# A hybrid encoder layer: the long convolution's decay window is read from a table in DRAM instead of being made on ScalarE

## The chip, the cores and the metric

The kernel runs on one core of one Trainium2 chip. The metric is the device time in microseconds of one execution. Of the kernel before, three executions took 3947.34, 3951.09 and 3955.97 us; the median is 3951.09 us.

The engines are named as the profile names them: PE is the matrix engine, with its weight loads shown apart as PEld; DVE is VectorE, ACT is ScalarE, POOL is GpSimd, and SP is the engine that issues most of the DMA transfers. Rows with the engine SPq or ACTq are DMA issues on those queues.

## The reference, cut to what matters

The layer projects 2048 tokens of 1024 channels, runs two token mixers side by side, a Hyena long convolution and an RWKV-7 scan, merges them with gates, normalises, and ends with a SwiGLU feed-forward part and a second normalisation. The change touches the Hyena filters alone:

```
t = jnp.linspace(0.0, 1.0, L)[:, None]
...                                   # a small sine network gives h: (L, 64)
h = (h @ fw4).reshape(L, HY_ORDER, 2, HY_WIDTH)
deltas = jnp.abs(jnp.linspace(HY_MIN_DECAY, HY_MAX_DECAY, HY_WIDTH))
window = jnp.exp(-t * deltas[None, :])
return h * window[:, None, None, :]
```

There are 2 orders, 2 directions and 512 channels. `window` depends on the position and the channel alone: on no input. `long_conv` convolves a signal of length 2048 with a forward and a backward filter by way of an FFT of length 4096, and adds `d_skip * z`, which the kernel folds into position 0 of the filter.

## The kernel before, in words

The program has these stages in order of time: the input projection with the preparation of the scan (to about 640 us), the scan in 64 chunk steps with the gate columns of the projection woven in (to about 1600 us), the long convolutions (to about 2110 us), the merge of the branches, and the feed-forward part (from about 2490 us). Dense products are made of three matmuls on split operands.

**The convolutions.** 512 channels make 4 blocks of 128, and each is convolved twice (order 0 and 1): eight products, in the order of the list `PRODUCTS`. For a product the filter's spectrum is made first, in eight chunks of four (128 x 128) pieces, by the generator `filters()`. For chunk q of a product:

- PE multiplies the sine network's output with the product's last weight matrix: tile `pg`, four matmuls of 128 x 128 (L1240; each is two passes, so a chunk shows as x8). In chunk 0 a row for the skip term is added (L1242).
- DVE multiplies `pg` with the window chunk, in place (L1244). This runs at raised priority.
- PE makes the first half of the Fourier transform of the result: tile `pf` (L1226, x8).
- ACT copies `pf` to SBUF (L1228) and stores it to the DRAM array `Hd` with a DMA on its own queue (L1229).

Each `yield` of the generator is a piece: "window product" and "transform of the chunk before" alternate, so that the transform of chunk q-1 follows the window product of chunk q. `upto(n)` runs the generator on. The window chunk itself is made on ACT by four exponentials of a row of deltas, each with its own scale column (L1214), one chunk ahead, in one of three buffers of 128 x 512 (ring places 8, 9 and 10).

**Who runs filters().** The first product's eight chunks, and two of the second, are made while the last steps of the scan run (steps 62 and 63) and just behind them; I call the stretch from 1540 to 1616 us the ramp. In it SP also loads the tables of the convolution (`open()` and `taken(k)`: `H3b`, the network's output, and `Fc`, the Fourier table, in four parts of 512 KB each, one part for two chunks), ACT and DVE run the scan's last normalisations (`normed`: squares L867, a root L868, a scaling L872) and the short convolutions (L1183, L1184, L1189). PE then turns the first signal (tile `ph` L1285) and transforms it (`pfz` L1294).

From 1616 us on, product k runs beside the filters of product k+1. A product has eight slots; in slot q PE makes `pz` from the signal's transform and `pz` from the next filter's (both L1309), DVE multiplies the first with the filter's spectrum (`H`, L1339) and with its swapped form (`Hs`, L1340), and PE adds up (`pq`, L1348 and L1349). `H` is a copy on ACT (L1325), and `Hs` is made from it by four small DMAs of 64 KB on SP (L1329, shown as `rg<-rg`). The filters' pieces (called F in `beside`) are put into slots 0, 1, 4, 5, 6 and 7. In slots 3 and 6 SP also reads half of the next product's spectrum back from DRAM (`Vf<-Hd`, L1319, four DMAs of 256 KB). The last filter piece is at about 2020 us.

**What sets the order.** In the scan the order of PE's instructions is written out by hand and the other engines are ordered by a scheduler; in the convolutions PE, ACT, DVE and SP all run in the order in which the code is written. Every DMA of SP and ACT signals one of eight semaphores in turn (named DMAHW0 to DMAHW7 in the program), and each DMA's issue waits until the DMA that last used its semaphore, eight places earlier in the two queues together, has landed.

Of the kernel before, what the change touches and what calls it, by code (L numbers as in the profile page):

```python
# [9 lines left out]
F32 = mybir.dt.float32  # L10
F32R = mybir.dt.float32r
AF = mybir.ActivationFunctionType
# [4 lines left out]
P = 128  # L17
# [5 lines left out]
HT = 4  # L23
# [16 lines left out]
PRODUCTS = [(c + k, o) for c in (0, 2) for o in range(2) for k in range(2)]  # L40
# [59 lines left out]
def shape_consts():  # L100
    f = np.float32
    F, G, M = fft_consts()
    Fz = np.concatenate([F[:64, 0::2], F[:64, 1::2]], 0)
    out = {"c_F": F, "c_Fz": Fz, "c_G": G, "c_M": M, "c_ident": np.eye(128)}
    p = np.arange(128)
    ind8 = np.zeros((128, HP, 8))
    for hp in range(HP):
        ind8[p, hp, hp * 2 + p // 64] = 1
    out["c_ind8"] = ind8
    out["c_ind8T"] = ind8.transpose(2, 1, 0)  # L110
    out["c_bones"] = (p[:, None] // 64 == p[None, :] // 64)
    sm = np.ones((128, 512))
    sm[:, ::CH] = 0
    out["c_smask"] = sm
    i = np.arange(64)
    row, col = i[:, None], i[None, :]

    mb = [row < col, row < col]
    mk = [row < col, row > 63 - col]
    rb = [row <= col, 63 - row >= col]  # L120
    rk = [row <= col, row >= col]
    even = lambda b, k: np.stack([np.concatenate([k[d], b[d]], 0) for d in range(2)], 1)
    odd = lambda b, k: np.stack([np.concatenate([b[d], k[d]], 0) for d in range(2)], 1)
    out["c_maskA"] = np.stack([even(mb, mk), odd(mb, mk)], 1)
    out["c_maskR"] = np.stack([even(rb, rk), odd(rb, rk)], 1)
    t = np.linspace(0.0, 1.0, L, dtype=f)
    w = (f(2.0 * math.pi) * np.arange(L, dtype=f) / f(L)).astype(f)
    fr = np.linspace(1e-4, 15, 16, dtype=f)
    ang = (w[:, None] * fr[None, :]).astype(f)
    feats = np.concatenate([t[:, None], np.cos(ang), -np.sin(ang)], -1).astype(f)  # L130
    n1, n2 = np.arange(64), np.arange(32)
    fwd = (32 * n1[None, :] + n2[:, None])
    bwd = 2048 - 32 * n1[None, :] - n2[:, None]
    bwd[0, 0] = 0
    out["c_feats"] = np.concatenate([feats[fwd.reshape(-1)].T, feats[bwd.reshape(-1)].T], 0)
    out["c_tcol"] = -np.concatenate([t[fwd].T, t[bwd].T], 0)
    mn, mx = math.log(1e-2) / 1.5, math.log(1e-2) / 0.3
    dl = np.abs(np.linspace(mn, mx, 512, dtype=f))
    out["c_delta"] = np.tile(dl[None], (128, 1))
    e0 = np.zeros((1, 128))  # L140
    e0[0, 0] = 1
    out["c_e0"] = e0
    return {k: np.ascontiguousarray(v, dtype=f) for k, v in out.items()}


# [1 line left out]
def lay_out(a):  # L147
# [36 lines left out]
    }  # L184
    o = {k: np.ascontiguousarray(v) for k, v in o.items()}
    o.update(shape_consts())
    return o

class Layer:
# [428 lines left out]


    def ring(self, k):
        return self.cm.tile([P, 512], F32, name="rg", tag=f"rg{k % 14}")

    def chain(self):
        tc, nc, i = self.tc, self.nc, self.i
# [2 lines left out]
        with tc.tile_pool(name="ch", bufs=1, reuse_waits="tile") as s, tc.tile_pool(name="chp", bufs=1, space=PSUM, reuse_waits="tile") as ps:  # L629
# [348 lines left out]
            def until(gen, n):  # L978
                for _ in range(n):
                    yield next(gen)  # L980
# [122 lines left out]
    def open(self):  # L1103
        nc, i = self.nc, self.i
        self.H3 = self.xp1.tile([P, 32, P], F32, name="H3b", tag="xh", bufs=1)
        self.Fc = self.xp1.tile([P, 32, P], F32, name="Fc", tag="xl", bufs=1)
        cu = self.wp.tile([P, 1026], F32, name="cu0", tag="wraw", bufs=2)
        self.Mc = self.wp.tile(self.i["c_M"].shape, F32, name="Mc", tag="wraw", bufs=2)
        self.Fz = [self.wp.tile([P, 8, P], F32, name="Fz", tag="wh", bufs=2) for k in range(2)]
        self.Gc = [self.wp.tile([P, 16, 64], F32, name="Gc", tag="wl", bufs=2) for k in range(2)]  # L1110
        self.turns = dict(w=0, A=0, B=0, H=0, Hs=0)
        self.smalls, self.pieces = {}, 0
        self.spots = [cu[:, 514:1026], self.ring(11)]
        self.tcol = self.load(self.fp, "c_tcol")
        self.e0 = self.load(self.fp, "c_e0")
        cw = self.load(self.fp, "conv")
        self.cw, self.cb = cw[:, :, 0:3], cw[:, :, 3]
        self.small(*PRODUCTS[0])
        self.taken(0)
        self.cus = [cu, self.wp.tile([P, 528], F32, name="cu1", tag="ex")[:, 0:514]]  # L1120
        self.conv, self.convs = self.shorts(), {}
        self.z0 = self.short(0)
        for k in range(2):
            nc.sync.dma_start(self.Fz[k], i["c_Fz"][:, 8 * k:8 * k + 8])
        nc.sync.dma_start(self.Mc, i["c_M"])
        for k in range(2):
            nc.sync.dma_start(self.Gc[k], i["c_G"][:, 16 * k:16 * k + 16])
# [5 lines left out]


    def next(self, name):
        first, n = dict(w=(8, 3), A=(12, 2), B=(0, 2), H=(2, 3), Hs=(5, 3))[name]
        k = self.turns[name]
        self.turns[name] = k + 1
        return self.ring(first + k % n).rearrange("p (a b) -> p a b", b=P)

    def small(self, c, o):
        nc, i = self.nc, self.i
        cs = slice(P * c, P * c + P)
        new = lambda n, sh: self.fp.tile(sh, F32, name=n, tag=n, bufs=2)
        fw4, delta, skip = new("fw4", [P, P]), new("delta", [P, P]), new("skip", [1, P])
        for d in range(2):
            nc.sync.dma_start(fw4[64 * d:64 * d + 64], i["fw4"][:, o, d, cs])
        nc.sync.dma_start(delta, i["c_delta"][:, cs])
        nc.sync.dma_start(skip, i["skip"][:, o, cs])
        self.smalls[c, o] = fw4, delta, skip  # L1150

# [52 lines left out]
    def filters(self):  # L1206
        nc = self.nc
        mm = nc.tensor.matmul
        ahead = None

        def window(delta, q):
            w = self.next("w")
            for j in range(4):
                nc.scalar.activation(w[:, j], delta, AF.Exp, scale=self.tcol[:, 4 * q + j:4 * q + j + 1])  # L1214
            return w

        for i, (c, o) in enumerate(PRODUCTS):
            fw4, delta, skip = self.smalls.pop((c, o))
            if i + 1 < 2 * HT:
                self.small(*PRODUCTS[i + 1])  # L1220

            def spec(q, g):
                ps, tag, bufs = self.fps
                p = ps.tile([P, 4, P], F32, name="pf", tag=tag, bufs=bufs)
                for j in range(4):
                    mm(p[:, j], self.Fc[:, 4 * q + j], g[:, j], start=True, stop=True)  # L1226
                u = self.spots[q % 2].rearrange("p (a b) -> p a b", b=P)
                nc.scalar.copy(u, p)  # L1228
                nc.scalar.dma_start(self.Hd[i, 4 * q:4 * q + 4].rearrange("n p c -> p n c"), u)  # L1229

            last = None
            for q in range(8):
                if ahead is None:
                    ahead = window(delta, q)
                g, ahead = ahead, None
                ps, tag, bufs = self.fps
                p = ps.tile([P, 4, P], F32, name="pg", tag=tag, bufs=bufs)
                for j in range(4):
                    n = 4 * q + j
                    mm(p[:, j], self.H3[:, n], fw4, start=True, stop=n != 0)  # L1240
                    if n == 0:
                        mm(p[:, j], self.e0[0:1], skip[0:1], start=False, stop=True)  # L1242
                with self.tc.high_priority(offset=2 * FIRST):
                    nc.vector.tensor_tensor(out=g, in0=p, in1=g, op=ALU.mult)  # L1244
                if q < 7:
                    ahead = window(delta, q + 1)
                elif i + 1 < 2 * HT:
                    ahead = window(self.smalls[PRODUCTS[i + 1]][1], 0)
                yield
                if q > 0:  # L1250
                    spec(q - 1, last)
                    yield
                last = g
            spec(7, last)
            yield
# [621 lines left out]
```

## Time and profile before

| what | value |
|---|---|
| median of three executions | 3951.09 us |
| the profiled execution, its own time | 3947.99 us |
| its span, first to last instruction | 3946.2 us |
| PE busy, DVE busy, ACT busy | 3801.3 us, 2346.6 us, 1456.8 us |
| exponentials of the window, L1214 | 256 instructions, 82.9 us on ACT |
| window products, L1244 | 64 instructions on DVE, 43.0 us |
| swapping DMAs, L1329 | 256 of 64 KB |
| HBM read, written | 369.52 MB, 144.70 MB |

The profile is of one execution, 3.1 us shorter than the median. A row of stages gives, for each engine, how long it was busy in a stretch of time, then the granted clock of PE as a share of full speed, the share of time that the DMA engines were busy, and the bytes moved in GB/s. A row of waits gives who waited for whom: the time in total, how often, and the longest. A row of the timeline gives start, duration, engine, line, operation and tiles, and in brackets the idle time ahead of it and what ended that.

### The profile page before, as it was taken

What the parts mean: (1) busy time and instruction counts of PE and PEld (TensorE: products, weight loads), DVE (VectorE), ACT (ScalarE), POOL (GpSimd) and SP (SyncE); (2) the same over time, 40 slices, a digit from 0 to 9 for tenths busy, and PEclk for the clock granted to TensorE, in tenths of its full rate; (3) what the DMA queues carried; (4) which work ended last, traced back from release to release, by engine and by line L of the source; (5) the groups of instructions that cost most, each with busy time, mean ns of one, the idle gap of its engine ahead of it and who ended that gap; (6) DMA issues with size and microseconds to landing.
All of it is one profiled execution on the core that took longest, in us unless ns stands there. A gap on an engine that the chain in (4) does not pass through costs nothing.

```text
span 3946.2 us, 64945 instructions
## 1 busy us (share of the span) xinstructions
PE 3801.3 (96%) x26152; PEld 3128.1 (79%) x26152; DVE 2346.6 (59%) x3734; ACT 1456.8 (37%) x2851; POOL 93.1 (2%) x139
## 2 busy tenths in 40 slices
PE   8999999999999998899988999999999999999998
PEld 6766557787777787899887999788888878888887
DVE  5466884666667775577676555544444474444444
ACT  3345663333335566655543333211111151111113
POOL 0000001111010100000000000000000000000000
PEclk9999999999999999899999999999999999999999
DMA  4556878677777777545555443411111142111111
GB/s 140 173 167 172 222 212 247 193 225 206 216 221 223 215 209 216 128 124 141 138 148 180 130 126 110 155 48 49 49 50 51 49 139 69 49 48 48 49 48 43
DMA packets 426420, 535.43 MB, mean 136 GB/s; under 512 B 137268, under 2 KB 305725, under 8 KB 423365
## 3 DMA queue, kind: packets, MB, share of 16 engines
q1 hardware_dynamic: 365703, 459.91, 40.1%
q10 hardware_dynamic: 54528, 54.59, 4.5%
q0 software_dynamic: 5888, 16.78, 1.6%
q8 instruction: 206, 3.38, 0.4%
q14 instruction: 95, 0.78, 0.1%
HBM read 369.52 MB, written 144.70 MB: 130 GB/s over the span
## 4 chain that ended last, share of the span: by engine, by line
PE 51%; DVE 3%; DMA 2%; ACT 1%; issue 1%; SPq 0%; ACTq 0%; DVEq 0%
PE pg L205 4%; PE pg L203 4%; PE pu L203 4%; PE pu L204 4%; PE pg L204 4%; PE pu L205 4%; PE pd L203 4%; PE pd L205 4%; PE pd L204 4%; PE pz L1309 2%; PE pm L203 1%; PE pm L204 1%; PE pm L205 1%; PE po L204 1%; PE po L205 1%; PE po L203 1%
## 5 line engine op out<-in xcount | busy, mean ns | idle before, releaser
L203 PE MATMUL acc<-xh,wh 128*128 128x512 f32 x1376 | 577.3, 420 | 9.4 <-ACT xh L198 8.4
L204 PE MATMUL acc<-xl,wh 128*128 128x512 f32 x1376 | 547.0, 398 | 3.9 <-DVE xl L199 3.8
L205 PE MATMUL acc<-xh,wl 128*128 128x512 f32 x1376 | 547.0, 398 | 0.8 <-DVE wl L199 0.8
L1814 DVE TENSOR_TENSOR acc<-pd,acc 128x1024 f32<-128x1024 f32 x320 | 387.6, 1221 | 69.3 <-PE pd L205 63.6
L198 ACT CAST fwh<-raw 128x1024 fp32r<-128x1024 f32 x132 | 138.6, 1050 | 704.6 <-PE pg L204 487.5
L203 PEld LDWEIGHTS acc<-xh,wh 128*128 128x128 f32 x1376 | 261.6, 190 | 120.4 <-issue 47.9
L1842 DVE TENSOR_TENSOR h<-pu,sg 128x512 f32<-128x512 f32 x88 | 60.9, 692 | 476.6 <-PE pu L205 470.8
L204 PEld LDWEIGHTS acc<-xl,wh 128*128 128x128 f32 x1376 | 262.3, 191 | 63.5 <-DVE xl L199 6.5
L205 PEld LDWEIGHTS acc<-xh,wl 128*128 128x128 f32 x1376 | 261.9, 190 | 62.6 <-DVE wl L199 2.1
L203 PE MATMUL pd<-fwh,hh 128*128 128x512 f32 x704 | 275.6, 391 | 2.8 <-DVE acc L1812 2.4
L205 PE MATMUL pd<-fwh,hl 128*128 128x512 f32 x704 | 274.9, 390 | 0.0
L204 PE MATMUL pd<-fwl,hh 128*128 128x512 f32 x704 | 274.8, 390 | 0.0
L203 PE MATMUL pu<-fxh,fwh 128*128 128x512 f32 x704 | 274.3, 390 | 0.5 <-ACT fxh L1728 0.5
L203 PE MATMUL pg<-fxh,fwh 128*128 128x512 f32 x704 | 274.1, 389 | 0.2 <-DVE fxl L1729 0.2
L205 PE MATMUL pg<-fxh,fwl 128*128 128x512 f32 x704 | 274.2, 389 | 0.0
L205 PE MATMUL pu<-fxh,fwl 128*128 128x512 f32 x704 | 274.1, 389 | 0.0
L204 PE MATMUL pu<-fxl,fwh 128*128 128x512 f32 x704 | 274.0, 389 | 0.0
L204 PE MATMUL pg<-fxl,fwh 128*128 128x512 f32 x704 | 273.9, 389 | 0.0
L199 DVE TENSOR_TENSOR fwl<-raw,fwh 128x1024 fp32r<-128x1024 f32 x132 | 161.1, 1221 | 166.6 <-ACT fwh L198 162.7
L199 DVE TENSOR_TENSOR wl<-wraw,wh 128x512 fp32r<-128x512 f32 (+1 forms) x217 | 169.3, 791 | 138.7 <-ACT wh L198 132.1
L198 ACT CAST wh<-wraw 128x512 fp32r<-128x512 f32 (+1 forms) x217 | 150.2, 704 | 221.2 <-PE acc L204 176.7
L203 PEld LDWEIGHTS pd<-fwh,hh 128*128 128x128 f32 x704 | 132.0, 188 | 41.0 <-DVE acc L1814 12.2
(290 smaller groups left out, 7490.4 us busy)
## 6 DMA issues: line engine op xcount, KB each, us to landing
wraw<-in_w_in SPq DMA_DIRECT2D x130, 512.0 KB
ABp<-ABd SPq DMA_DIRECT2D x64, 512.0 KB
raw<-in_fg SPq DMA_DIRECT2D x44, 512.0 KB
raw<-in_fu SPq DMA_DIRECT2D x44, 512.0 KB
raw<-in_fd SPq DMA_DIRECT2D x44, 512.0 KB
ud<-ev ACTq DMA_DIRECT2D x84, 256.0 KB
ABd<-AB SPq DMA_DIRECT2D x32, 512.0 KB
gated<-ev SPq DMA_DIRECT2D x64, 256.0 KB
```

Of the source, the lines that this page charges most:

```text
L198: nc.scalar.copy(hi, src)
L199: nc.vector.tensor_tensor(out=lo, in0=src, in1=hi.bitcast(F32), op=ALU.subtract)
L203: mm(ps, ah, bh, start=start, stop=False)
L204: mm(ps, ah, bl, start=False, stop=False)
L205: mm(ps, al, bh, start=False, stop=stop)
L1309: mm(p[:, j], Mc[:, 0 if 4 * q + j == 0 else 3], v[:, j], start=True, stop=True)
L1814: tt(out=acc[t], in0=pf, in1=acc[t], op=ALU.add)
L1842: tt(out=h, in0=put, in1=sg, op=ALU.mult)
```

## The change

The window is computed on the host from constants alone and passed as a DRAM array `c_win` of 4 x 128 x 32 x 128 numbers (8.4 MB); `filters()` reads chunk q of channel block c from it with one DMA of 256 KB on SP (128 rows of 2 KB). The first two chunks are asked for at the generator's start, and then the window product of a chunk is followed by the DMA for the chunk two further on; the list `todo` runs over all 64 chunks without a break between products. There are four buffers in place of three: ring place 14, which nothing used before, is the fourth. The window's 256 exponentials, the scale columns (`c_tcol`), the deltas (`c_delta`, one small DMA for each product) and the row `c_e0` with a single 1 go; row 0 of the identity stands in for the last.

```
-    out["c_tcol"] = -np.concatenate([t[fwd].T, t[bwd].T], 0)
+    tcol = -np.concatenate([t[fwd].T, t[bwd].T], 0)
...
-    out["c_delta"] = np.tile(dl[None], (128, 1))
-    e0 = np.zeros((1, 128))
-    e0[0, 0] = 1
-    out["c_e0"] = e0
+    out["c_win"] = np.exp(tcol[None, :, :, None] * dl.reshape(4, 1, 1, 128))
...
     def ring(self, k):
-        return self.cm.tile([P, 512], F32, name="rg", tag=f"rg{k % 14}")
+        return self.spot(k % 14)
+
+    def spot(self, k):
+        return self.cm.tile([P, 512], F32, name="rg", tag=f"rg{k}")
...
-        first, n = dict(w=(8, 3), A=(12, 2), B=(0, 2), H=(2, 3), Hs=(5, 3))[name]
+        spots = dict(w=(8, 9, 10, 14), A=(12, 13), B=(0, 1), H=(2, 3, 4), Hs=(5, 6, 7))[name]
...
-        nc.sync.dma_start(delta, i["c_delta"][:, cs])
...
-        def window(delta, q):
+        def window(c, q):
             w = self.next("w")
-            for j in range(4):
-                nc.scalar.activation(w[:, j], delta, AF.Exp, scale=self.tcol[:, 4 * q + j:4 * q + j + 1])
-            return w
+            nc.sync.dma_start(w, self.i["c_win"][c, :, 4 * q:4 * q + 4])
+            ahead.append(w)
+
+        for _ in range(2):
+            window(*todo.pop(0))
...
             for q in range(8):
-                if ahead is None:
-                    ahead = window(delta, q)
-                g, ahead = ahead, None
+                g = ahead.pop(0)
...
                     if n == 0:
-                        mm(p[:, j], self.e0[0:1], skip[0:1], start=False, stop=True)
+                        mm(p[:, j], self.ident[0:1], skip[0:1], start=False, stop=True)
...
-                if q < 7:
-                    ahead = window(delta, q + 1)
-                elif i + 1 < 2 * HT:
-                    ahead = window(self.smalls[PRODUCTS[i + 1]][1], 0)
+                if todo:
+                    window(*todo.pop(0))
```

PE's instructions stand in the same order in both programs. The two queues that change are ACT and SP.

ACT in the ramp, kernel before: between the third and the fourth copy of a transform (`cu<-pf`, `rg<-pf`, L1228) stand the last step's squares (`sq`), roots (`vr`) and scalings (`y`), the window's exponentials (`rg<-delta`) and the changes of ACT's function table.

```order
L1228 COPY cu_16347<-pf 128x512
L1214 ACT_TABLE_LOAD
L1214 ACTIVATE rg<-delta,k_c_tcol 128x128
L891 ACTIVATE yo<-pgt,k_gn_b,k_gn_w 128x64 x2
L867 ACTIVATE sq,vr<-y,nm 128x64 x4
L1229 DMA Hd<-cu_16347 128x4x128
L868 ACT_TABLE_LOAD
L868 ACTIVATE vr<-vr,eps 128x4
L1214 ACT_TABLE_LOAD
L1214 ACTIVATE rg<-delta,k_c_tcol 128x128
L872 ACTIVATE y<-y,nm,vr 128x64 x4
L1228 COPY rg<-pf 128x512
```

The same two copies in the changed kernel (line numbers shift by a few):

```order
L1228 COPY cu_16347<-pf 128x512
L1229 DMA Hd<-cu_16347 128x4x128
L892 ACTIVATE yo<-pgt,k_gn_b,k_gn_w 128x64 x2
L1228 COPY rg<-pf 128x512
L1229 DMA Hd<-rg 128x4x128
```

All exponentials of the window and, over the whole program, 13 of the 48 table loads of ACT are gone (the seven ahead of L1214 and six of the seven ahead of L868), and one is new ahead of a later activation.

SP in the ramp, kernel before: parts 3 and 4 of `H3b` and `Fc` with the scan's last loads (`A`, `gs`, `bn`, `y`).

```order
L915 DMA yrd<-yo 128x4x128
L1131 DMA H3b<-H3d 128x1024
L1132 DMA Fc<-in_c_F 128x1024
L778 DMA A_4634<-ABd 64x4x64 x2
L898 DMA gs<-gsd 128x128
L900 DMA bn<-bond 128x4x128
L859 DMA y<-Yd 128x256
L1131 DMA H3b<-H3d 128x1024
L1132 DMA Fc<-in_c_F 128x1024
L859 DMA y<-Yd 128x256
```

The same place in the changed kernel:

```order
L916 DMA yrd<-yo 128x4x128
L1211 DMA rg<-in_c_win 128x512
L1130 DMA H3b<-H3d 128x1024
L1131 DMA Fc<-in_c_F 128x1024
L779 DMA A_4634<-ABd 64x4x64 x2
L899 DMA gs<-gsd 128x128
L901 DMA bn<-bond 128x4x128
L860 DMA y<-Yd 128x256
L1211 DMA rg<-in_c_win 128x512 x2
L1130 DMA H3b<-H3d 128x1024
L1211 DMA rg<-in_c_win 128x512
L1131 DMA Fc<-in_c_F 128x1024
```

One window read stands ahead of part 3, two more ahead of part 4 of `H3b`, and a fourth between it and part 4 of `Fc`. The windows of chunks 0 to 3 are read earlier, during the scan, and those of chunks 8 to 11 between these rows and the first `Vf<-Hd`. In the convolutions proper 52 window reads stand between the swaps, each behind the transform (on PE) of the chunk whose buffer it takes.

More of the change, by code (lines that the diff above doesn't have):

```diff
@@ L1113, in open @@
         self.spots = [cu[:, 514:1026], self.ring(11)]
-        self.tcol = self.load(self.fp, "c_tcol")
-        self.e0 = self.load(self.fp, "c_e0")
         cw = self.load(self.fp, "conv")
@@ L1135, in next @@
     def next(self, name):
-        first, n = dict(w=(8, 3), A=(12, 2), B=(0, 2), H=(2, 3), Hs=(5, 3))[name]
+        spots = dict(w=(8, 9, 10, 14), A=(12, 13), B=(0, 1), H=(2, 3, 4), Hs=(5, 6, 7))[name]
         k = self.turns[name]
         self.turns[name] = k + 1
-        return self.ring(first + k % n).rearrange("p (a b) -> p a b", b=P)
+        return self.spot(spots[k % len(spots)]).rearrange("p (a b) -> p a b", b=P)
     def small(self, c, o):
@@ L1144, in small @@
         new = lambda n, sh: self.fp.tile(sh, F32, name=n, tag=n, bufs=2)
-        fw4, delta, skip = new("fw4", [P, P]), new("delta", [P, P]), new("skip", [1, P])
+        fw4, skip = new("fw4", [P, P]), new("skip", [1, P])
         for d in range(2):
             nc.sync.dma_start(fw4[64 * d:64 * d + 64], i["fw4"][:, o, d, cs])
-        nc.sync.dma_start(delta, i["c_delta"][:, cs])
         nc.sync.dma_start(skip, i["skip"][:, o, cs])
-        self.smalls[c, o] = fw4, delta, skip
+        self.smalls[c, o] = fw4, skip
     def shorts(self):
@@ L1208, in filters @@
         mm = nc.tensor.matmul
-        ahead = None
-        def window(delta, q):
+        ahead, todo = [], [(c, q) for c, o in PRODUCTS for q in range(8)]
+        def window(c, q):
             w = self.next("w")
-            for j in range(4):
-                nc.scalar.activation(w[:, j], delta, AF.Exp, scale=self.tcol[:, 4 * q + j:4 * q + j + 1])
-            return w
+            nc.sync.dma_start(w, self.i["c_win"][c, :, 4 * q:4 * q + 4])
+            ahead.append(w)
+        for _ in range(2):
+            window(*todo.pop(0))
         for i, (c, o) in enumerate(PRODUCTS):
-            fw4, delta, skip = self.smalls.pop((c, o))
+            fw4, skip = self.smalls.pop((c, o))
             if i + 1 < 2 * HT:
```

## The prediction

> **What bounds the kernel now.** I read the page's busy shares first, then the stretches of time, then who PE waits for in each, then the chain of waits of the two stretches in which the window is made.
>
> ```profile
> span 3946.2 us, 64945 instructions
> PE 3801.3 (96%) x26152; PEld 3128.1 (79%) x26152; DVE 2346.6 (59%) x3734; ACT 1456.8 (37%) x2851; POOL 93.1 (2%) x139
> ...
> 1400.00:1540.00 140.00, 138.76 (x1746) 113.67 (x1746) 90.85 (x240) 93.36 (x273) 6.88 (x10) 0.99 0.69 187
> 1540.00:1616.00 76.00, 57.68 (x507) 51.12 (x504) 35.20 (x74) 55.14 (x141) 0.00 (x0) 0.77 0.70 200
> 1616.00:2030.00 414.00, 393.46 (x3582) 376.77 (x3583) 291.81 (x329) 234.82 (x504) 0.00 (x0) 0.99 0.52 133
> 2030.00:2112.00 82.00, 66.74 (x584) 62.94 (x583) 60.67 (x65) 26.15 (x43) 0.00 (x0) 0.92 0.45 129
> ```
>
> PE is busy nearly throughout, so work taken off ACT is worth only the PE time that waits for it, or that runs at a low clock because of it. In the scan (first stage) PE idles 1.2 of 140 us. In the ramp it idles 18.3 of 76 us and its clock is 0.77. In the convolutions proper it idles 20.5 of 414 us. The last stage holds no window. So the change can act in the ramp and in the 414 us behind it, and nowhere else; in the scan I put it at nothing.
>
> In the ramp the idle time has a shape:
>
> ```profile
> 1556.49 1.38 PE L1240 MATMUL pg<-fw,H3b 128*128 128x128 f32 x8 [3.68 <-DMA H3b<-H3d]
> ...
> 1580.11 2.08 PE L1240 MATMUL pg<-fw,H3b 128*128 128x128 f32 x8 [3.57 <-ACT rg L1228]
> ...
> 1588.44 2.07 PE L1226 MATMUL pf<-rg,Fc 128*128 128x128 f32 x8 [2.65 <-ACT cu L1228]
> 1591.85 2.05 PE L1226 MATMUL pf<-rg,Fc 128*128 128x128 f32 x8 [1.33 <-DVE rg L1244]
> ```
>
> Up to about 1570 us PE waits for transfers and for the scan's chain; from 1575 on it waits for ACT's copies of the transforms, or for a window product that waits for its exponentials. ACT is full there. The next three rows are of 1570 to 1595 us: all of ACT, then L1214 alone, then the roots' line L868 alone.
>
> ```profile
> 1570.00:1595.00 25.00, 24.05 (x62) 0.72 0.52 157
> 1570.00:1595.00 25.00, 10.19 (x21) 0.72 0.52 157
> 1570.00:1595.00 25.00, 3.16 (x4) 0.72 0.52 157
> ...
> L1214 ACT ACTIVATE rg<-delta,k_c_tcol 128x128 f32<-128x128 f32 x48 | 16.5, 395 | 0.5
> L1214 ACT ACT_TABLE_LOAD x7 | 9.0, 1283 | 0.1
> L868 ACT ACT_TABLE_LOAD x6 | 7.7, 1283 | 0.1
> ```
>
> The last three rows are of 1400 to 1620 us. Exponential and root need different tables, and the two alternate, so each pays a load of 1.28 us.
>
> **The change part by part.** *ACT, ramp.* Of ACT's 24.05 us from 1570 to 1595 go L1214's 10.19 (exponentials and three loads) and the two loads on L868, 2 x 1.28 = 2.57: 12.8 us, half of it. A backlog of that size cannot stay: the copies that PE waited for 3.57 and 2.65 us follow their transforms directly (the rows of the order show it), and the 1.33 us behind a late exponential becomes a wait for a transfer. But something is late next, and it is H3b. SP's issues and PE's product from the third part:
>
> ```profile
> 1549.39 0.43 SPq L1131 DMA_DIRECT2D H3b<-H3d  x1
> ...
> 1560.24 0.50 SPq L1131 DMA_DIRECT2D H3b<-H3d  x1
> ...
> 1567.64 0.45 SPq L1131 DMA_DIRECT2D H3b<-H3d  x1
> ...
> 1567.79 1.06 PE L1240 MATMUL pg<-fw,H3b 128*128 128x128 f32 x8
> ...
> 1560.00:1565.00 5.00, 3.14 (x52) 2.82 (x50) 1.68 (x4) 3.49 (x13) 0.00 (x0) 0.84 0.99 297
> 1570.00:1575.00 5.00, 4.29 (x57) 3.91 (x57) 2.56 (x7) 4.95 (x15) 0.00 (x0) 1.00 0.98 317
> 1575.00:1580.00 5.00, 1.16 (x8) 0.97 (x8) 1.87 (x7) 4.96 (x12) 0.00 (x0) 0.77 0.49 140
> ```
>
> Part 2, issued at 1549.39, released PE at 1556.49: 7.1 us for 512 KB with the DMA engines nearly full, as they are to 1575. Part 4 went out at 1567.64; two window reads now stand ahead of it, at 0.45 us an issue, so say 1568.5, landing 7.1 us later, 1575.6. With the third part's read, three windows of 256 KB are in front of it: 0.75 MB at 317 GB/s is 2.5 us, so 1578. The product of 1580.11 therefore starts 2 us earlier, not 3.57. Behind it the waits of 2.65 and 1.33 us and a small one of 0.4 go: 4.4. Together 6.4 us. Bounds: 2 us, if the reads hold up Fc's fourth part (one more window ahead of it) as well; 8.9 us, all that PE idles from 1575 to 1600, if the transfers overlap better than in sequence. The delay of part 3 by one read, 0 to 3.5 us (half of 7.1), I take as inside the 2.5.
>
> *The clock in the ramp.*
>
> ```profile
> 1575.00:1600.00 25.00, 16.06 (x78) 14.38 (x78) 9.40 (x21) 19.83 (x51) 0.00 (x0) 0.66 0.37 107
> 1600.00:1616.00 16.00, 14.76 (x89) 13.30 (x90) 1.91 (x3) 8.66 (x19) 0.00 (x0) 0.66 0.74 165
> ...
> 1605.00:1610.00 5.00, 5.00 (x25) 4.11 (x25) 0.00 (x0) 2.36 (x5) 0.00 (x0) 0.50 1.09 248
> 1610.00:1615.00 5.00, 5.00 (x31) 5.00 (x31) 0.00 (x0) 1.93 (x4) 0.00 (x0) 0.50 0.87 184
> ```
>
> PE works 30.8 us at a clock of 0.66; at full clock that is 30.8 x 0.66 = 20.3 us. So 0 to 10.5 us can be won where the idle gaps go. The rows argue for less than half: from 1605 to 1615 PE has no gap and still runs at 0.50. I take 4. Ramp: 6.4 + 4 = 10.4 us.
>
> The Trainium skill (TensorE: Matmul & The Clock Gate, Part 1: The HAM clock gate) has it that the matrix engine starts at half clock and gets the full clock after a busy window of about 3.4 us. The two rows just shown are against it for this kind of matmul: ten busy us at 0.50. By the rule, closing the gaps would bring back all of it; that is the first rival below.
>
> *ACT, convolutions proper.* What PE waits for in 1616 to 2030 us:
>
> ```profile
> PE pg L1240 <- ACT cu L1228: 4.1, 6, 0.7
> PE pg L1240 <- DVE rg L1244: 2.9, 3, 1.1
> PE pf L1226 <- DVE rg L1244: 1.5, 1, 1.5
> ...
> PE pg L1240 <- ACT rg L1228: 0.7, 1, 0.7
> ...
> L1214 ACT ACTIVATE rg<-delta,k_c_tcol 128x128 f32<-128x128 f32 x212 | 67.7, 391 | 8.6 <-ACT rg L1228 4.5 <-ACT cu L1228 4.0
> ```
>
> ACT loses 67.7 us of 234.8, a quarter, but it idles 43% here. Only copies that stand directly behind four exponentials (4 x 0.32 = 1.3 us) hold PE: 4.1 + 0.7 = 4.8 us. I take 4. The DVE rows are DVE's own queue (transposes ahead of the window product) and stay.
>
> *SP and the transfers.* Added are 64 reads of 256 KB, 16.8 MB, 52 of them behind 1616 us; gone are eight small loads. By bytes there is room: 133 GB/s moved there, and 13.6 MB over 414 us adds 33. By the queue it is closer:
>
> ```profile
> SPq L1329 <- DMA Hd<-rg: 67.1, 17, 6.1
> ...
> SPq L1329 <- DMA Hd<-cu: 33.2, 14, 4.7
> ...
> DVE rg L1340 <- DMA rg<-rg: 11.0, 9, 2.4
> ...
> PE pz L1309 <- DVE rg L1340: 2.7, 2, 2.4
> ...
> 1666.18 4.11 DMA Hd<-cu
> ...
> 1803.54 1.06 PE L1240 MATMUL pg<-fw,H3b 128*128 128x128 f32 x8
> 1811.62 1.06 PE L1240 MATMUL pg<-fw,H3b 128*128 128x128 f32 x8
> ```
>
> SP's swaps wait 100.3 us, 31 times, for a spectrum store that used their semaphore eight places before: 3.2 us each. They are just in time: DVE waits 11.0 us for swaps, and PE 2.7 us for that. A window read now stands in this queue. Its lead is two chunks: the products of chunks 5 and 7 of one product are 8.1 us apart, and with the matmuls of 0.9 us DVE needs the window 9.0 us after it was asked for. A read behind four swaps (2.4), one such wait (3.2) and its own landing (4.1, by a store of the same size on the chain) takes 9.7 us: late by 0.7. Most reads have less ahead of them, and the stores themselves leave 1.3 us earlier where exponentials stood ahead of the copy. The queue behind a read is the next swaps, whose copies on ACT are not yet there when it waits for PE, so that wait costs them nothing. I take a loss of 3 us, about 2.7 us of PE waits doubled; bounds: 0, and 30 (third rival).
>
> *The sum.* 10.4 + 4 - 3 = 11.4 us off the profiled execution's 3947.99 us (1.8 us of it around the span): 3936.6. That execution is 3.1 us below the median of the runs shown, so I forecast 3939.7 for the median, 3940 rounded: 0.28% faster.
>
> **The rivals.**
>
> *The clock comes back in full.* All gaps from 1575 to 1600 close (8.9 us) and the stretch to 1616 runs at full clock (10.5), with 4.8 us behind it: 24 us, 3927. For it: at 1570 to 1575, when PE had work, the clock was 1.00. Against it: the rows at 0.50 above.
>
> *ACT was not the limit that counts.* The ramp's transfers are: the DMA engines are at 0.98 until 1575, and another 2.1 MB (chunks 4 to 11) at 317 GB/s is 6.6 us. Then part 4 and Fc come as late as ACT's copies did, the ramp wins its lower bound of 2 us, and with 4 - 3 us behind it the change gives 3 us: 3948, no difference. For it: the full DMA rows, and that the exponentials themselves are hardly waited for. Against it: the share falls to 0.49 after 1575, just where ACT is full.
>
> *Slower: the windows come late.* The place is DVE's window product in the slots around each `Vf<-Hd`, two in each of seven products. If a read is behind the longest wait (6.1) it takes 2.4 + 6.1 + 4.1 = 12.6 us, 3.6 too late; behind the mean one 0.7; in the middle 2.1. DVE runs in order, so its transposes and products for PE come late by as much: 14 x 2.1 = 30 us. Less the ramp's 10.4 and the 4 this is 15 us slower: 3966. It decides from the point where SP lags by more than 9.0 - 4.1 = 4.9 us behind the code. Against it: PE loses only 2.7 us to the swaps that stand in the same queue today.
>
> **How the numbers follow.** My forecast has 0.52; the clock rival 0.13; transfers instead of ACT 0.21; late windows 0.14. The forecast's own range is 3932 to 3947 (ramp 5 to 15 us, the rest plus or minus 4). Over all the range is 3927 to 3960. A difference of 0.2%, 7.9 us, is about what a measurement of this kernel can tell. Below 3943.2 lies most of the forecast (0.42 of 0.52) and the clock rival: faster 0.55. The rest of the forecast and the transfer rival, less a little: same 0.30. The late windows and a little of the others: slower 0.15.
>
> **What would show it.** Right: no PE wait for L1228 between 1570 and 1600, ACT well under 0.7 busy there, `ph` (1601.02 before) about 7 to 9 us earlier, and the first `pz` about 10 earlier; instead a wait of PE for H3b's fourth part or of DVE for a window near 1578. A clock of 0.9 and more through the ramp would speak for the first rival. Waits of DVE's window product for the window's DMA, above 5 us in all behind the ramp, would speak for the third, and an unchanged `ph` for the second. I would be wrong outright if the time moved before 1540 or after 2112 us, where nothing is costed.

## The result, and the profile after the change

The changed kernel takes 3993.24 us, the median of four executions (3983.76 to 3996.04), against 3949.22 us for the kernel before. The ratio is 1.0117, with a 95% interval of 1.0098 to 1.0136: 44 us slower, where 11 us faster was forecast. The range, 3927 to 3960, does not hold it.

First the head of the changed kernel's page, then three stretches of it, each cut at the same PE instructions as the three of before in the prediction: the ramp to the first `pz`, the convolutions proper (414 us before), and the last stage.

```profile
span 3991.9 us, 64786 instructions
PE 3818.2 (96%) x26152; PEld 3135.5 (79%) x26152; DVE 2347.2 (59%) x3734; ACT 1365.3 (34%) x2583; POOL 93.0 (2%) x139
```

```profile
1538.00:1601.00 63.00, 48.12 (x502) 42.75 (x502) 34.45 (x74) 35.84 (x100) 0.00 (x0) 0.89 0.90 263
1601.00:2061.00 460.00, 409.23 (x3588) 389.80 (x3587) 292.70 (x329) 173.89 (x293) 0.00 (x0) 0.96 0.57 150
2061.00:2142.00 81.00, 66.13 (x581) 62.48 (x580) 60.27 (x65) 27.11 (x43) 0.00 (x0) 0.94 0.45 129
```

ACT lost its 91 us, as planned, and the ramp got shorter: 63 us instead of 76. But the convolutions proper take 460 us instead of 414. PE idles 50.8 us there (460 - 409.23) where it idled 20.5, and the same number of matmuls keeps it busy 15.8 us longer, at a clock of 0.96 instead of 0.99. The two together are the 46 us by which the stage grew.

To place all of the difference, I took the start of the same PE instruction from two traces. The table gives how much longer (+) or shorter (-) each stretch is than in the first profile of before, in us; its columns are named by that profile's times, and 1618 is the first filter matmul behind the first eight `pz`. Rows e1 to e10 are the experiments of the next section; "before, again" is a second profile of the unchanged kernel, so its row shows what a difference means.

| kernel | to 1470 | 1470 to 1540 | ramp, to 1618 | 1618 to 2044 | 2044 to 2490 | 2490 to 3880 |
|---|---|---|---|---|---|---|
| before, again (e5) | -1.6 | +1.6 | -6.4 | +2.0 | +1.4 | +2.6 |
| changed | -4.4 | +2.1 | -13.2 | +46.4 | -1.8 | +16.7 |
| changed, again (e6) | -9.3 | +0.4 | -14.4 | +47.9 | +2.3 | +12.6 |
| e1, reads on POOL | -11.3 | +5.1 | -17.2 | +3.0 | -2.5 | +13.5 |
| e2, one resident window | -9.5 | +5.1 | -18.0 | -2.3 | +1.3 | +14.2 |
| e3, exponentials and reads | -15.8 | -0.8 | -4.4 | +8.1 | -0.7 | +14.8 |
| e4, reads of a quarter | -9.1 | +1.7 | -16.4 | +21.7 | -1.0 | +13.8 |
| e7, stores on POOL | -10.3 | +5.1 | -14.6 | +2.1 | +1.7 | +12.8 |
| e8, changed + 1664 bytes | -6.9 | -0.4 | -7.7 | +45.5 | -1.9 | +0.6 |
| e9, e1 + 1664 bytes | -12.1 | +2.4 | -17.1 | +0.3 | -0.5 | -0.5 |
| e10, e7 + 1664 bytes | -8.4 | +7.7 | -12.7 | +1.8 | -1.8 | +0.6 |

By the mean of the two profiles on each side the change costs 46.2 us in the convolutions and 13.4 us in the feed-forward part, wins 10.6 us in the ramp and 6 us ahead of 1470, and is within 0.5 us elsewhere: 43 us together, close to the 44 measured. So there are two losses to explain, and one lies in a stage whose code was not touched.

**Where the convolutions lose.** Waits of DVE, of SP's queue and of PE in the changed kernel (time in total, how often, longest; those of PE behind the ramp, those of SP behind 1616 us), and one of before that the prediction did not show:

```profile
DVE rg L1242 <- DMA rg<-in_c_win: 54.7, 15, 8.0
...
SPq L1325 <- DMA Hd<-rg: 52.1, 11, 7.1
...
SPq L1211 <- DMA Hd<-cu: 12.8, 4, 6.4
...
PE po L1354 <- DVE V L1299: 13.4, 4, 4.2
PE pz L1305 <- DVE V L1299: 10.8, 6, 2.8
PE pf L1226 <- DVE rg L1242: 9.4, 5, 2.2
PE pg L1238 <- ACT rg L1228: 7.4, 11, 0.7
PE pg L1238 <- ACT cu L1228: 4.1, 6, 0.7
PE pg L1238 <- DVE rg L1242: 3.2, 4, 1.1
```

```profile
PE pz L1309 <- DVE V L1303: 7.7, 6, 2.9
```

The window product (L1242) waits 54.7 us for its read, all 15 times behind the ramp, which ends at 1601 us here; nine of the times are in chunks 6 and 7 of a product. DVE's transposes (L1299) stand behind the product in its order and come late too (in the case below the next one starts at 1826.53, just behind the late product), and PE's waits for DVE grow from 12.1 us (7.7, 2.9 and 1.5) to 36.8. Why the read is late is seen in one case, the timeline of the changed kernel around chunk 7 of the fifth product, in order of time:

```profile
1811.31 0.64 DVE L1242 TENSOR_TENSOR rg<-pg,rg 128x512 f32<-128x512 f32 x1
...
1814.01 0.64 DVE L1242 TENSOR_TENSOR rg<-pg,rg 128x512 f32<-128x512 f32 x1
...
1815.55 1.06 PE L1226 MATMUL pf<-rg,Fc 128*128 128x128 f32 x8
...
1816.65 0.58 ACT L1228 COPY rg<-pf 128x512 f32<-128x512 f32 x1 [0.30 <-PE pf L1226]
1817.26 0.37 ACTq L1229 DMA_DIRECT2D Hd<-rg  x1
...
1821.55 0.51 SPq L1325 DMA_DIRECT2D rg<-rg  x1
1822.16 1.02 SPq L1211 DMA_DIRECT2D rg<-in_c_win  x2
...
1825.92 0.69 DVE L1242 TENSOR_TENSOR rg<-pg,rg 128x512 f32<-128x512 f32 x1 [7.95 <-DMA rg<-in_c_win]
...
1828.85 3.42 PE L1354 MATMUL po<-V,Gc 128*64 128x128 f32 x32 [4.19 <-DVE V L1299]
```

The rows are the products of chunks 5 and 6, the transform of chunk 5, its copy, its store, a swap on SP, the read for chunk 7 (with the next read behind it, hence x2), the product of chunk 7, and PE's next matmuls behind it. The swap shares its semaphore with the store and goes out 4.3 us after it (1821.55 after 1817.26); the read for chunk 7 stands behind the swap and lands 3.8 us later. The prefetch of two chunks has become a chain: product of chunk 5, transform, copy, store, swap, read, product of chunk 7, 14.6 us in all, where the kernel before goes from product 5 to product 7 in 7.0 us (the starts of its products in the same place are 2.7 and 4.3 us apart).

Then PE stands still for 4.19 us, and its clock falls:

```profile
1825.00:1830.00 5.00, 1.16 (x12) 1.19 (x14) 3.92 (x4) 0.38 (x1) 0.00 (x0) 0.84 0.64 186
1830.00:1835.00 5.00, 5.00 (x49) 4.83 (x46) 2.60 (x4) 2.47 (x4) 0.00 (x0) 0.82 0.01 3
```

From 1830 to 1835 it works without a gap at 0.82. In this stage PE has nine gaps of over 2 us; before it had one. By the clock's own records PE works 31 us of the stage at 0.50, against 6 us before, which costs 12.6 of the 15.8 us; where the other 3 us come from I could not see.

The Trainium skill (TensorE: Matmul & The Clock Gate, Part 1: The HAM clock gate) has the clock fall back after an idle window of about 3.4 us; the row after this gap of 4.19 us agrees. But six of the eight falls in this stage come with shorter gaps, of 1.83 to 3.12 us, while other gaps of up to 2.73 us have none. One of each:

```profile
1889.10 1.40 PE L1226 MATMUL pf<-rg,Fc 128*128 128x128 f32 x8 [1.86 <-DVE rg L1242]
1889.90:1893.20 3.30, 3.30 (x18) 3.30 (x17) 2.49 (x2) 2.13 (x4) 0.00 (x0) 0.50 0.52 129
...
1734.37 0.79 PE L1305 MATMUL pz<-V,Mc 128*128 128x128 f32 x5 [2.73 <-DVE V L1299]
1734.40:1739.40 5.00, 5.00 (x45) 5.00 (x46) 3.83 (x6) 1.17 (x2) 0.00 (x0) 1.00 0.99 259
```

**Where the feed-forward part loses.** The same group of matmuls between 2600 and 3900 us, before and after (count, busy us, mean ns of one):

```profile
L203 PE MATMUL pg<-fxh,fwh 128*128 128x512 f32 x640 | 249.1, 389 | 0.0
```

```profile
L201 PE MATMUL pg<-fxh,fwh 128*128 128x512 f32 x624 | 245.1, 393 | 0.0
```

PE idles no more than before (some 4 us of the stage in both), the granted clock is 1.00 in both, and a matmul takes about 1% longer on average. By the starts of the gate and up products between 2800 and 3800 us, 691 of 2714 follow their predecessor by 235 ns or more after the change, and none of 2758 before; the mean rises from 226.7 to 230.1 ns. The slow ones are every second matmul in half of the products: those whose moving tile is the first of the two input tiles. That tile belongs to a pool opened ahead of all the removed ones and lies at the same address in both programs; what has moved in these products is the weights.

### The profile page after: what moved, and what is told of

Read it like the earlier page. It is cut to its first block, busy times and chain, and to the rows that moved or that the text cites. A ratio compares the mean times of both kernels' runs of the same rounds, so it can differ in the third digit from the quotient of the medians.

```text
span 3991.9 us, 64786 instructions
## 1 busy us (share of the span) xinstructions
PE 3818.2 (96%) x26152; PEld 3135.5 (79%) x26152; DVE 2347.2 (59%) x3734; ACT 1365.3 (34%) x2583; POOL 93.0 (2%) x139
## 4 chain that ended last, share of the span: by engine, by line
PE 47%; DVE 3%; DMA 3%; ACT 1%; issue 0%; SPq 0%; ACTq 0%; DVEq 0%
PE pg L203 4%; PE pg L201 4%; PE pg L202 4%; PE pu L201 4%; PE pu L203 4%; PE pu L202 4%; PE pd L203 4%; PE pd L202 4%; PE pd L201 4%; PE pm L201 1%; PE pm L202 1%; PE pm L203 1%; PE po L203 1%; PE po L202 1%; PE po L201 1%; PE pz L1305 1%
```

## The experiments

In all, three theories of the late windows were tested (L, T and Q, stated with e1), and two of the slow matmuls (A and C, stated with e8). Each batch ran beside executions of the kernel before on its own chip, and ratios are against those.

**e1: the reads on POOL's queue.**

```
-            nc.sync.dma_start(w, self.i["c_win"][c, :, 4 * q:4 * q + 4])
+            nc.gpsimd.dma_start(w, self.i["c_win"][c, :, 4 * q:4 * q + 4])
```

> The 64 window reads go out on POOL's queue instead of SP's; same bytes, same lead of two chunks, same four buffers. Theory L (a closed loop: on SP a read stands behind a swap that waits for the spectrum store of the chunk before, so each late window makes the next one late): the window product's waits for the read fall from 54.7 us to under 10 us, the loss of 41 us between the products from 1640 to 2050 us goes, the time is 3930 to 3945 us. Theory T (16.8 MB more on the DMA engines slow all transfers): the reads still take long, time 3975 to 3995 us. Theory Q (64 more issues keep SP busy, and the swaps go out late): as L, 3935 to 3950 us.

Measured: 3940.31 us, ratio 1.0014 (1.0003 to 1.0026). The window product's waits, all of them:

```profile
its engine sat idle before it (us, times) until:
  PE pg L1238: 9.6, 12
```

No wait for a read is left, and of the 46 us in the convolutions 3 remain. The bytes are the same, so theory T falls. SP's swaps still wait for the stores (63.9 and 47.1 us), but no window read stands behind them. Yet the kernel is only level with the one before, which pointed to the second loss.

**e2: one window chunk for all products.**

```
+        one = self.spot(14).rearrange("p (a b) -> p a b", b=P)
+        nc.sync.dma_start(one, self.i["c_win"][0, :, 0:4])
...
-                    nc.vector.tensor_tensor(out=g, in0=p, in1=g, op=ALU.mult)
+                    nc.vector.tensor_tensor(out=g, in0=p, in1=one, op=ALU.mult)
```

> One window chunk is read once and used for all 64 products (the other 63 chunks are left out); the exponentials stay away. It prices what ACT's relief is worth with no transfer at all. All theories: no wait for a window; the ramp as in the changed kernel or 2 to 6 us better, some 5 us less behind it: 3925 to 3937 us. If this is not faster than the kernel before, ACT's relief was worth nothing.

Measured: 3936.21 us, ratio 0.9989 (0.9978 to 1.0000): at the upper end of what was expected, since the feed-forward part costs 14.2 us here too. PE's waits for ACT's copies in its convolutions, with no exponential and no read in the program's way:

```profile
PE pg L1231 <- ACT cu L1221: 4.1, 6, 0.7
...
PE pg L1231 <- ACT rg L1221: 0.7, 1, 0.7
```

They are to the digit those of before. So they are not waits behind exponentials. The convolutions win 2.3 to 4.3 us at most (-2.3 against 0 and +2.0), and not by less waiting. The stage from 1618 to 2044 in e2 and in before, cut at the same instructions:

```profile
1595.20:2019.80 424.60, 397.67 (x3647) 380.96 (x3645) 304.73 (x342) 179.01 (x302) 0.00 (x0) 1.00 0.54 136
```

```profile
1617.60:2044.40 426.80, 400.16 (x3646) 383.09 (x3644) 304.50 (x342) 241.29 (x515) 0.00 (x0) 0.99 0.52 135
```

PE idles 26.9 us in e2 and 26.6 before; the difference is in the time that it works, at a clock of 1.00 and 0.99.

**e3: exponentials kept, and the reads made as well.**

```
+        def idle(c, q):
+            w = self.spot(14).rearrange("p (a b) -> p a b", b=P)
+            nc.sync.dma_start(w, self.i["c_win"][c, :, 4 * q:4 * q + 4])
...
+                nc.scalar.activation(w[:, j], self.ident, AF.Exp, scale=self.cw[:, j, 1:2])
...
+                if todo:
+                    idle(*todo.pop(0))
...
```

> The exponentials stay on ACT (of a constant tile in place of the deltas, so the window's values are left out) and the 64 reads of 256 KB are made on SP as well, into one buffer that nothing reads. It prices issues and transfers without anyone waiting for them. Theory L: 3945 to 3960 us, hardly slower than the kernel before. Theory T and theory Q: 3970 to 3995 us, and DVE's waits for the swaps (11.0 us before) rise to 30 us or more.

Measured: 3956.03 us, ratio 1.0047 (1.0031 to 1.0062), of which 12 us lie in the feed-forward part (14.8 against 2.6 for before, again). The convolutions are 6 to 8 us longer, not 46. DVE's waits for swaps rise, as T and Q had it:

```profile
DVE rg L1346 <- DMA rg<-rg: 39.9, 16, 5.8
```

So 64 issues and 16.8 MB on SP do delay the swaps, but that is worth a sixth of the loss. It takes someone waiting for the reads to lose the rest.

**e4: reads of a quarter.** One piece of 64 KB is read and used for all four.

```
-            nc.sync.dma_start(w, self.i["c_win"][c, :, 4 * q:4 * q + 4])
+            w = self.cm.tile([P, P], F32, name="wq", tag=f"wq{q % 4}")
+            nc.sync.dma_start(w, self.i["c_win"][c, :, 4 * q])
...
-                g = ahead.pop(0)
+                w, g = ahead.pop(0), self.next("w")
...
```

> As the changed kernel, but each read is a quarter (64 KB, one of four pieces, used for all four; the other three pieces are left out). Theory L: the wait for the store stays and only the read's own landing gets shorter (3.7 to about 2 us): of the 41 us lost between 1640 and 2050 us half or more stays, 3965 to 3985 us. Theory T: a quarter of the loss stays, 3945 to 3958 us. Theory Q: as the changed kernel, 3980 to 3995 us.

Measured: 3958.01 us, ratio 1.0059 (1.0040 to 1.0078). In the convolutions 21.7 of 47 us stay, a little under the half that L expected and well over T's quarter; SP's swaps wait as long as ever, and the products wait 35.2 us:

```profile
SPq L1325 <- DMA Hd<-rg: 60.7, 16, 6.7
...
DVE rg L1242 <- DMA wq<-in_c_win: 35.2, 11, 6.4
```

Its time lies at the upper end of T's range and below L's. But it holds the 13.8 us of the feed-forward part that neither knew of, and the kernel before was 10 us faster beside it (3939 us) than beside the changed kernel. By itself this run would not decide; it fits a chain in which the read's landing is one link.

**e5 and e6: both kernels once more.**

> The kernel before once more, for a second profile of it: the stages of other runs are read against two profiles instead of one. All theories: 3930 to 3955 us; the ramp as in the first profile, first pz about 76 us after 1540, if its low clock there is a property of the kernel and not of that one execution.

> The changed kernel once more beside the others. All theories: 1.0 to 1.3% slower than the kernel before; 15 waits of the window product for its read, 50 to 60 us in all, at chunks 2, 6 and 7 of each product.

Measured: 3947.61 us in one execution, and 3988.57 us with a ratio of 1.0118 (1.0097 to 1.0139). The changed kernel's window product waits for its read again, 14 times and 50.4 us, again most often in chunks 6 and 7. The ten microseconds at a clock of 0.50 in the prediction, and the same work in the second profile of before:

```profile
1605.00:1615.00 10.00, 10.00 (x54) 9.11 (x55) 0.00 (x0) 4.29 (x9) 0.00 (x0) 0.50 0.98 216
```

```profile
1604.10:1609.80 5.70, 5.58 (x53) 4.93 (x54) 0.00 (x0) 4.02 (x8) 0.00 (x0) 1.00 1.05 240
```

The same work runs at a clock of 1.00: the 0.50 belonged to that one execution. Of the 13.8 us that the ramp seemed to win against the first profile, 5.4 us are that spell.

**e7: reads on SP, stores on POOL.** This takes the store out of the rotation that SP's DMAs share.

```
-                nc.scalar.dma_start(self.Hd[i, 4 * q:4 * q + 4].rearrange("n p c -> p n c"), u)
+                nc.gpsimd.dma_start(self.Hd[i, 4 * q:4 * q + 4].rearrange("n p c -> p n c"), u)
```

> As the changed kernel, window reads on SP, but the spectrum stores (Hd) go out on POOL's queue instead of ACT's, so that no DMA of SP has a store eight places before it. Theory L (the loop closes through the semaphore that a swap shares with the store of the chunk before): SP's waits for Hd (100 us) go, the window product's waits for its read fall from 54.7 to under 10 us, 3930 to 3950 us. Theory T (transfers) and theory Q (too many issues on SP): the windows stay late, 3970 to 3995 us.

Measured: 3945.10 us, ratio 1.0011 (0.9997 to 1.0025). What SP's swaps and half-spectrum reads wait for now, and what the window product waits for:

```profile
SPq L1325 <- ACT rg L1321: 67.6, 27, 6.1
...
SPq L1315 <- DMA Hd<-rg: 10.9, 3, 3.9
```

```profile
  DMA rg<-in_c_win: 1.9, 3
```

The swaps no longer wait for a store (the 10.9 us are the read-back of data just stored), the reads stand in the same queue with the same neighbours, and they are on time. Theory Q falls, and L is shown: the loop closes through the semaphore shared with the store. My wording "the store of the chunk before" was loose; the trace has the read of chunk q+2 behind the store of chunk q.

**e8: the changed kernel with its feed-forward tiles moved back.** The removed small tiles (two of 512 bytes for the deltas, 512 for `c_e0`, 128 for `c_tcol`) had moved all later tiles down by 1664 bytes per partition. One unused tile undoes that for the last stages; every engine's order stays as it was.

```
                     with tc.tile_pool(name="mf", bufs=1, reuse_waits="tile") as self.mf:
-
+                        self.mf.tile([P, 416], F32, name="pad", tag="pad")
```

> The changed kernel with an unused tile of 1664 bytes per partition ahead of the feed-forward stage's tiles, so that they lie at the addresses that they have in the kernel before (the change took 1664 bytes of small tiles away and moved everything behind them). No instruction and no order differs. Theory A (addresses: every second matmul of a quarter of the feed-forward part takes 237 ns instead of 227 because of where its tiles lie): from 2490 to 3880 us the 13 us that all changed kernels lost there come back, 3970 to 3980 us. Theory C (the chip's clock, or chance): no difference to the changed kernel, 3984 to 3994 us.

Measured: 3973.33 us, ratio 1.0079 (1.0063 to 1.0095). The group shown above, in this kernel:

```profile
L201 PE MATMUL pg<-fxh,fwh 128*128 128x512 f32 x633 | 246.4, 389 | 0.0
```

It is at 389 ns again, and none of 2752 starts is 235 ns or more behind its predecessor. From 2490 us on it is 0.6 us from before instead of 13 to 17. Theory A is shown: where the tiles lie in SBUF is worth 14 us here, and 12 to 14 us in the next two runs.

**e9 and e10: both cures together.** Each is e1 or e7 with the line of e8.

> Both cures: window reads on POOL's queue, and the tile of 1664 bytes. Theory A: 3926 to 3933 us, 0.2 to 0.4% faster than the kernel before. Theory C: as the reads on POOL alone, 3936 to 3945 us, no difference to the kernel before.

> Window reads on SP, spectrum stores on POOL's queue, and the tile of 1664 bytes. Theory A: 3930 to 3937 us, 0.1 to 0.3% faster than the kernel before. Theory C: as the stores on POOL alone, 3940 to 3950 us.

Measured: e9 3926.43 us, ratio 0.9965 (0.9953 to 0.9977); e10 3929.77 us, ratio 0.9965 (0.9952 to 0.9979). Both are faster than the kernel before by about 0.35% and than the change by about 1.5%, as theory A had it (e10 comes out just under its range). The head of e9's page:

```profile
span 3918.3 us, 64822 instructions
PE 3777.7 (96%) x26152; PEld 3112.4 (79%) x26152; DVE 2345.4 (60%) x3734; ACT 1364.5 (35%) x2583; POOL 127.4 (3%) x203
```

So without its two losses the change is worth 14 us; what stood against it was the queue that the reads used and the bytes that were freed. How much of the 14 us is ACT's relief is not shown: in e9's profile the ramp is 10.7 us shorter than in the second profile of before, and the stretch to 1470, where the change was expected to do nothing, another 10.5 us.

## Why the prediction was wrong, step by step

**The ramp: right in its sum, not in its parts, and by another limit.** Forecast were 10.4 us; the means of two profiles give 10.6. Cut at the first `pz`, PE's idle time falls from 17.8 and 17.1 us to 14.7 and 13.4, by 3.4 where 6.4 were forecast; its working time falls from 57.3 and 52.6 us to 48.3 twice, by 6.6, where the clock term was 4. ACT's backlog went as said:

```profile
1570.00:1595.00 25.00, 18.68 (x157) 16.63 (x157) 12.34 (x27) 13.95 (x44) 0.00 (x0) 0.93 0.86 258
```

ACT is busy 13.95 of 25 us (24.05 before). But `H3b`'s fourth part did not become the limit. It went out at 1567.42, and its product started at 1573.57 with no wait, 6.2 us later and 6.5 us ahead of before. What stops PE now are the scan's own last steps on ACT:

```profile
1573.57 1.06 PE L1238 MATMUL pg<-fw,H3b 128*128 128x128 f32 x8
...
1580.18 2.05 PE L1226 MATMUL pf<-rg,Fc 128*128 128x128 f32 x16 [2.10 <-ACT yo L892]
...
1589.67 2.04 PE L913 MATMUL pgg<-gs,k_g 128*128 128x128 f32 x8 [2.19 <-ACT yo L892]
```

The term of 4 us for the clock rested on rows of one execution that do not repeat (e5), so that the sum agrees is luck. e3 bounds what ACT's relief gave: with the exponentials kept the ramp is only as in "before, again" (-4.4 against -6.4), without them it is 6 to 12 us shorter than that in every run but e8, whose ramp has a spell of 0.50 like the first profile's.

**The convolutions, ACT's term: wrong, all 4 us of it.** The 4.1 and 0.7 us that PE waits for copies were read as waits behind four exponentials. They stayed in e2, and in the changed kernel they are 4.1 and 7.4: a wait for a copy is also there when no exponential stands ahead of it.

**The convolutions, SP's term: this is the step that failed.** It was put at a loss of 3 us, and the stage lost 46. "A read behind four swaps (2.4), one such wait (3.2) and its own landing (4.1) takes 9.7 us: late by 0.7." The mean wait of a swap was put in as if it were independent of the reads and spread over all swaps. In the trace the swap ahead of the read for chunk q+2 waits for the store of chunk q, whose product the read follows in the code; a product that is late makes the store, the swap and the next read late. The wait to put in was from the product to its store's landing, 10.2 us (1811.31 to 1821.55), not 3.2; with a swap's issue (0.6) and the read (3.8) that makes the 14.6. The lead was too long as well: 9.0 us were taken from PE's rows, and on DVE the two products are 7.0 us apart. The price of the transfers and issues alone is about twice the 3 us that I took: e3 gives 6 to 8 us, and e1 less e2 5.3 us.

**The third rival had the mechanism, its side and its place**: DVE's product late in two slots of a product, around `Vf<-Hd`, with its chance at 0.14; its sign, waits of more than 5 us, came with 54.7. It counted 14 delays of 2.1 us, 30 us; the trace has 15 waits of 3.6 us each. And it left out the clock: PE loses 30 us more in gaps than before, and 12.6 by working slowly behind them. What I held against it, that PE loses only 2.7 us to the swaps of today, was no evidence: those swaps have no one waiting for them in a loop.

**Outside the stages costed.** "I would be wrong outright if the time moved before 1540 or after 2112 us." It did: behind 2112 us it lost 13 us, through addresses, and ahead of 1540 it won some 6. A change that takes tiles away moves every tile allocated behind them; no step asked what that does. Without it the change would have measured 1.0079, still beyond the range.

**The other two rivals** (the clock comes back in full, transfers bound the ramp) were about the ramp alone, and neither decided. The first came in part: the ramp's clock is 0.89 and 0.92 in the two profiles of the changed kernel, where its sign was 0.9, against 0.77 and 0.85 in the two of before. The sign of the second, an unchanged `ph`, did not come: `ph` starts at 1591.50 instead of 1601.02.

**What stays open.** Why every second matmul is slower with the weights at the one address and not at the other was not tried; only the two layouts were. All ten profiles of kernels whose tiles moved are 4 to 16 us shorter up to 1470 us, against 1.6 us for the second profile of before. That may be addresses too, since the tiles of those stages moved as well (e8 to e10 put back only the last stages'), but no run separates it, and it may be the execution or the chip: the kernel before itself took 3939 to 3942 us beside e1 to e10, against 3949 beside the changed kernel. From 1470 to 1540 us some lose 5 to 8 us and the others 2.4 at most; in e1 PE stands still there for 4.4 us with nothing in the profile to wait for, in e2 for 1.9 us behind a small transfer, and I did not follow it up. Nor did I follow why PE's waits for ACT's copies into `rg` grow from 0.7 us to 7.4 in the changed kernel and 7.8 in e7, when e1 and e2 have 0.7.

## What to carry to other kernels

A prefetch's lead counts only if nothing ahead of it in its queue waits, directly or through a shared semaphore, for the work that the prefetch feeds: follow the queue and the rotation back from the read, and if they meet its consumer, put read or store on another queue. When a stage that was not edited changes speed with no wait and the same clock, compare the spacing of its matmuls and the addresses of its tiles, and try an unused tile. Price gaps of PE of about two microseconds and more with the slow clock that can follow them, here 12.6 us on 30.

## What the runs showed of the hardware

Moving the feed-forward tiles by 1664 bytes per partition, the weights among them, made a quarter of the gate and up products start 235 ns or more after their predecessor instead of some 227, 12 to 14 us in 1400; moving them back undid it. In the ramp PE ran ten microseconds and more without a gap at a granted clock of 0.50 in two of twelve profiles (the first of before, and e8), and at 1.00 over the same work in the second profile of before; what sets it off does not show in the traces. And in the changed kernel's convolutions the clock fell to 0.50 behind gaps of PE as short as 1.83 us, but not behind every gap of 2 to 3 us.
